# Fetching spilled results earlier, and one weight sum made by an accumulating DMA, in a two-layer float32 encoder

## The chip, the cores and the metric

The kernel runs on one core of a Trainium2 chip. The metric is the device time of one execution in microseconds (us). TensorE (PE in the profile) does the matmuls, with its weight loads shown as PEld; VectorE is DVE, ScalarE is ACT, GpSimd is POOL and SyncE is SP. SP, ACT and POOL also issue DMAs, each in the order of its own instruction queue; an engine that has reached an instruction whose inputs are missing waits there, with everything queued behind it.

## The reference, cut to what matters

Two layers over 256 rows of 2048 channels in float32. Per layer one input projection gives all branches; the branches are gated, projected, mixed and put through an output projection with a residual.

```
h = rmsnorm(x, norm_w)
proj = h @ w_in          # q_m k_m v_m z_m o_m g_m q_r k_r v_r z_r gate_m gate_r
h_m = mlstm(q_m, k_m, v_m, gates), both directions
u_m = head_rmsnorm(sigmoid(o_m) * h_m) * silu(z_m)
h_r = retention(rope(q_r), rope(k_r), v_r), both directions
u_r = head_rmsnorm(h_r) * silu(z_r)
mix = sigmoid([gate_m, gate_r] + b_mix)
y = mix[:D] * (u_m @ w_proj_m) + mix[D:] * (u_r @ w_proj_r)
x = x + y @ w_out
```

## The kernel before, in words

**Matmuls.** Every float32 operand is split into a high part that TensorE takes as it is and a remainder; a product is three matmuls (high by high, high by low, low by high; `mm3`, L270 to L273). Weights stream from DRAM in pieces of 128x1024 (512 KB): `wload` issues the DMA on SP into one of 7 `raw` tiles, `wsplit` lets ScalarE write the high part `whi` (L262) and VectorE the remainder `wlo` (L263), both into one pool of 12 `w` tiles. `gemm` (L332) is one product of 256 rows by 512 columns: 8 pieces of 12 matmuls each.

**Side work.** Seven pairs of 512-column blocks per layer (o_m, gate_m, half of z_r, gate_r) are not done by `gemm` but by `seven` (L411), which needs seven half-size products in the place of eight (a Strassen scheme). Its items are fed out beside the main gemms, by weights: `side_chunk` (L321) is called after each piece of a gemm and takes items until its share of the total weight is reached. Items p1, p5, p6 and p7 load the weight pieces r11, r12 and r22 and make three sums of them on VectorE: r11+r12 in place, that plus r22 into one of the four slices of the tile `keep` (L445), and r12+r22. After `middle` the items p2, p3 and p4 load r21 (and r22 again); p4 adds r21 into the slice of `keep` (the fourth sum, `wsum`, L268) and multiplies with it. `middle` and `end` combine the products, and `finish` applies the gate: for gate_m and gate_r it loads a row of `b_mix` into a `row` tile (2 of them, shared with the decay rows `dec` of the retention) by a DMA on ACT's queue.

**Spills.** Results that are needed later go to DRAM: `spill` (L97) is a DMA on POOL's queue, `fetch` (L102) one on SP's queue into one of 7 tiles of 128x512 (`t512`), which most small steps share.

**Order.** A compiler pass places the instructions of each engine by priority: an instruction's place in the program, less the offset of `tc.high_priority`. Loads, fetches and weight splits carry 800 (`AHEAD`); the vector and scalar operations named `vec` and `sca` carry 1600 (`URGENT`). `later` queues the small steps, and `run_later` takes one step of them at each piece of a gemm from number `lead` on (3 unless said). In the stage of the z_m gemms (named zm) the queue holds `gated` (the product of h_m and sigmoid(o_m), its mean square) and `um_chunk` (transposes of the gated result for the next product). The gemms named pj are the two projections, zr are the direct half of z_r, wo the output projection.

Of the kernel before, what the change touches and what calls it, by code (L numbers as in the profile page):

```python
# [16 lines left out]
P = 128  # L17
# [44 lines left out]
def encoder_kernel(ctx: ExitStack, tc: tile.TileContext, x, x_t, positions, w_main, w_qk0, w_qk1, b_mgate, vecs, b_mix,  # L62
# [12 lines left out]
    def bank(name):  # L75
        return pg.tile([P, 512], F32, name=name, tag="bank")
# [331 lines left out]
            yield  # L408
        side_start(make_items(s_hi=s_hi, s_lo=s_lo, keep=bigt("keep", 4)), 20 * NCK)

    def seven(l, xop, s_hi, s_lo, keep, blk, finish):  # L411

        def sop(i, kt):
            o = (i * HK + kt) * P
# [14 lines left out]
        def p1(i):  # L429
            if i == 0:  # L430
                for name in "abcd":
                    st["ps_" + name] = bank("s" + name)
            load("r11", 0, i)
            load("r12", 1, i)
            load("r22", 1, HC + i)
            product(st["ps_a"], lambda kt: xop(0, kt), st["r11"], i, True, True)
# [5 lines left out]
        def p6(i):  # L442
            with tc.high_priority(offset=AHEAD):
                t2 = keep[:, i * CW:(i + 1) * CW]
                nc.vector.tensor_tensor(out=t2, in0=st["r11"], in1=st["r22"], op=ALU.add)  # L445
            product(st["ps_b"], lambda kt: sop(1, kt), t2, i, True, True)

        def p7(i):
            wsum(st["r12"], st["r12"], st["r22"])
# [14 lines left out]
        def p2(i):  # L464
            if i == 0:
                for name in "acd":
                    st["ps_" + name] = bank("r" + name)
            load("r21", 0, HC + i)
            load("r22", 1, HC + i)
            product(st["ps_a"], lambda kt: xop(0, HK + kt), st["r21"], i, True, True)  # L470
# [3 lines left out]

        def p4(i):
            t2 = keep[:, i * CW:(i + 1) * CW]
            wsum(t2, t2, st["r21"])
            product(st["ps_d"], lambda kt: xop(1, HK + kt), t2, i, True, True)

        def end():  # L480
# [13 lines left out]
                items.append((w, lambda fn=fn, i=i: fn(i)))  # L494
        items.append((2.0, middle))
        for i in range(HC):
            for w, fn in ((0.5, p2), (0.5, p3), (1.6, p4)):
                items.append((w, lambda fn=fn, i=i: fn(i)))
        items.append((1.5, end))
        return items  # L500
# [263 lines left out]
    for l in range(DEPTH):  # L764
# [53 lines left out]

        def side_items(l=l, xop=xop, rs=rs, s_hi=None, s_lo=None, keep=None):
            def finish_with(kind, b0):  # L820
                def finish(t, n, src, own):
                    sg = t512(kind) if own is None else own
                    b = b0 + n
                    if kind in ("om", "zr"):
                        sca.activation(out=sg, in_=src, func=AF.Sigmoid if kind == "om" else AF.Silu, scale=rs[t])
                    else:
                        bm = row("bm")
                        mc = (0 if kind == "gm" else D) + b * NB
                        with tc.high_priority(offset=AHEAD):
                            nc.scalar.dma_start(out=bm, in_=b_mix[l:l + 1, mc:mc + NB].broadcast_to([P, NB]))  # L830
                        vec.scalar_tensor_tensor(out=sg, in0=src, scalar=rs[t], in1=bm, op0=ALU.mult,
                                                       op1=ALU.add)
                        sca.activation(out=sg, in_=sg, func=AF.Sigmoid)
                    spill((kind, l, b, t), sg)
                return finish
            items = []
            for kind, base, b in (("om", B_O_M, 0), ("om", B_O_M, 2), ("gm", B_GATE, 0), ("gm", B_GATE, 2),
                                  ("zr", B_Z_R, 0), ("gr", B_GATE + NBLK, 0), ("gr", B_GATE + NBLK, 2)):
                items += seven(l, xop, s_hi, s_lo, keep, base + b, finish_with(kind, b))
            return items  # L840

        for b in range(NBLK):
# [49 lines left out]
        um = []  # L892

        def gated(h, hs, ss):
            for t in range(NT):
                hv = fetch(("hm", l, h, t), "hm_b")
                so = fetch(("om", l, h, t), "so_b")
                vec.tensor_tensor(out=hv, in0=hv, in1=so, op=ALU.mult)
                sca.activation(out=so, in_=hv, func=AF.Square, accum_out=ss[:, t:t + 1])
                hs.append(hv)  # L900
                yield
            rstd_m = sm.tile([P, NT], F32, name="rstd_m")
            rsqrt_mean(rstd_m, ss, NT, NB)
            hs.append(rstd_m)
# [4 lines left out]
        for b in range(NBLK):  # L909
            side_need(("om", l, b, 1))  # L910
            side_need(("om", l, b, 0))
            hs = []
            ss_m = sm.tile([P, NT], F32, name="ss_m")
            later(gated, b, hs, ss_m)
            ps = gemm(xop, wmain(l, B_Z_M + b), "zm")
            while len(hs) <= NT:
                run_later()
            rstd_m = hs[NT]
            ev = []
            for t in range(NT):  # L920
                z = t512("z")
                sca.activation(out=z, in_=ps[t], func=AF.Silu, scale=rs[t])
                vec.scalar_tensor_tensor(out=z, in0=hs[t], scalar=rstd_m[:, t:t + 1], in1=z,
                                               op0=ALU.mult, op1=ALU.mult)
                ev.append(z)
            later(um_chunk, ev, b)
# [4 lines left out]

        uop = lambda t, kt: in_acts(um)(t, kt)
        for b in range(NBLK):
            ps = gemm(uop, wmain(l, B_PROJ_M + b), "pj")
            for t in range(NT):
                side_need(("gm", l, b, t))
                sg = fetch(("gm", l, b, t), "gm_b")
                vec.tensor_tensor(out=sg, in0=ps[t], in1=sg, op=ALU.mult)
                spill(("ym", l, b, t), sg)

# [2 lines left out]
        def ur_chunk(b, zs):  # L943
            ev = []
            hrs = [fetch(("hr", l, 2 * b + k), "hr_b") for k in range(2)]
            for t in range(NT):
                z = fetch(("zr", l, b, t), "z_b") if zs is None else zs[t]
                for k in range(2):
                    i = t * NH_R + 2 * b + k
                    zk = z[:, k * S:(k + 1) * S]  # L950
                    vec.scalar_tensor_tensor(out=zk, in0=hrs[k][:, t * S:(t + 1) * S], scalar=rstd_r[:, i:i + 1],
                                             in1=zk, op0=ALU.mult, op1=ALU.mult)
                ev.append(z)
            if zs is None:
                yield
            ur[b] = transpose_split(ev, b, None, None, (l, V_RN))
            yield

# [24 lines left out]
        for b in range(NBLK):  # L983
            if b == 2:
# [2 lines left out]
                y_hi, y_lo = bigt("y_hi", 2, F32R), bigt("y_lo", 3, F32R)  # L987
                later(y_chunk, None, 0)
                later(y_chunk, None, 1)
            ps = gemm(rop, wmain(l, B_PROJ_R + b), "pj", lead=2)  # L990
            ev = []
            for t in range(NT):
                side_need(("gr", l, b, t))
                sg = fetch(("gr", l, b, t), "gr_b")
                ym = fetch(("ym", l, b, t), "ym_b")
                vec.tensor_tensor(out=sg, in0=ps[t], in1=sg, op=ALU.mult)
                vec.tensor_tensor(out=sg, in0=ym, in1=sg, op=ALU.add)
                ev.append(sg)
# [181 lines left out]
```

## Time and profile before

| what | value |
|---|---|
| median of 3 runs | 2194.8 us (2194.19 to 5458.12) |
| the profiled execution | 2194.46 us |
| its span, first to last instruction | 2192.4 us |
| TensorE busy | 2154.0 us, 98% of the span |
| VectorE busy | 1813.4 us, 83% |
| ScalarE busy | 1304.3 us, 59% |
| GpSimd busy | 66.9 us, 3% |
| mean DMA rate | 236 GB/s, 518.25 MB moved |

The profiled execution is the one to which the rows below belong; 2.1 us of its time lie outside its span. Matmuls are pipelined, so one matmul's duration in the profile is longer than the distance from its start to the next one's; TensorE's pace is read from the starts.

### The profile page before, as it was taken

To read this page: it belongs to the slowest core of one execution; us is meant where nothing else is said; L and a number is where in the kernel's file an instruction comes from. 1 tells how busy PE (TensorE), PEld (TensorE's weight loads), DVE (VectorE), ACT (ScalarE), POOL (GpSimd) and SP (SyncE) were. 2 spreads that over 40 slices of the span, in tenths; PEclk is the share of its full clock that TensorE was granted. 3 is DMA by queue.
4 is the path that set the end of the run, shared out by engine and by line. 5 is a ranking of instruction groups with operands and counts; after the bars stand their busy time and mean duration, and the time that the engine had idled before them with its cause. 6 is when DMAs were issued, how large, how long until landed. Compare 5 with 4: busy or idle time off the path is not lost.

```text
span 2192.4 us, 28486 instructions
## 1 busy us (share of the span) xinstructions
PE 2154.0 (98%) x10024; PEld 1809.9 (83%) x10024; DVE 1813.4 (83%) x2327; ACT 1304.3 (59%) x1627; POOL 66.9 (3%) x130
## 2 busy tenths in 40 slices
PE   7999999999999999999999999999999999999998
PEld 7988888888778888888899888888887788888887
DVE  6997898897898998985578778989978989889854
ACT  6745466656775656564457555665567656565543
POOL 0000000000000000000000000000000000000000
PEclk9999999999999999999999999999999999999999
DMA  8645577767777887887656456776777778878963
GB/s 277 213 150 190 191 236 236 229 229 241 241 241 264 280 283 258 271 295 276 221 168 208 164 185 210 236 234 216 240 247 239 255 255 292 280 252 277 326 223 125
DMA packets 161071, 518.25 MB, mean 236 GB/s; under 512 B 19616, under 2 KB 22176, under 8 KB 160928
## 3 DMA queue, kind: packets, MB, share of 16 engines
q1 hardware_dynamic: 143552, 471.98, 65.4%
q0 software_dynamic: 9600, 31.46, 3.6%
q10 hardware_dynamic: 7776, 13.00, 2.0%
q8 instruction: 78, 1.28, 0.2%
q14 instruction: 65, 0.53, 0.1%
HBM read 482.81 MB, written 33.55 MB: 236 GB/s over the span
## 4 chain that ended last, share of the span: by engine, by line
issue 48%; PE 42%; DVE 3%; DMA 3%; POOL 2%; ACT 1%; SPq 0%; ACTq 0%; POOLq 0%; DVEq 0%
PE pj L272 3%; PE pj L273 3%; PE pj L271 3%; DVE wlo L263 2%; PE vm L271 1%; PE vm L272 1%; PE wo L273 1%; PE wo L272 1%; PE wo L271 1%; PE vr L271 1%; PE vr L272 1%; PE qr L271 1%; PE vm L273 1%; PE qr L273 1%; PE vr L273 1%
## 5 line engine op out<-in xcount | busy, mean ns | idle before, releaser
L262 ACT CAST whi<-raw 128x1024 fp32r<-128x1024 f32 (+2 forms) x832 | 844.6, 1034 | 608.1 <-DVE raw L268 147.7
L263 DVE TENSOR_TENSOR wlo<-raw,whi 128x1024 fp32r<-128x1024 f32 (+2 forms) x832 | 981.0, 1200 | 214.7 <-ACT whi L262 200.1
L272 PE MATMUL pj<-wlo,u_hi 128*128 128x512 f32 x512 | 199.4, 390 | 0.6 <-DVE wlo L263 0.5
L271 PE MATMUL pj<-whi,u_hi 128*128 128x512 f32 x512 | 199.9, 391 | 0.0
L273 PE MATMUL pj<-whi,u_lo 128*128 128x512 f32 x512 | 199.3, 389 | 0.0
L262 ACT CAST whi<-keep 128x1024 fp32r<-128x1024 f32 x112 | 117.7, 1051 | 60.0 <-PE qr L272 12.8
L263 DVE TENSOR_TENSOR wlo<-keep,whi 128x1024 fp32r<-128x1024 f32 x112 | 136.4, 1218 | 15.7 <-ACT whi L262 15.1
L268 DVE TENSOR_TENSOR raw<-raw 128x1024 f32<-128x1024 f32 x112 | 136.4, 1218 | 0.8
L271 PE MATMUL qk<-whi,ht_hi 128*128 128x384 f32 (+2 forms) x320 | 113.7, 357 | 10.5 <-ACT whi L262 10.5
L272 PE MATMUL qk<-wlo,ht_hi 128*128 128x384 f32 (+2 forms) x320 | 113.4, 354 | 1.0 <-DVE wlo L263 1.0
L272 PEld LDWEIGHTS pj<-wlo,u_hi 128*128 128x128 f32 x512 | 96.1, 188 | 21.0 <-DVE wlo L263 1.5
L273 PE MATMUL qk<-whi,ht_lo 128*128 128x384 f32 (+2 forms) x320 | 113.0, 353 | 0.0
L273 PEld LDWEIGHTS pj<-whi,u_lo 128*128 128x128 f32 x512 | 96.1, 188 | 20.0
L271 PEld LDWEIGHTS pj<-whi,u_hi 128*128 128x128 f32 x512 | 96.0, 188 | 20.0 <-ACT whi L262 0.4
L272 PE MATMUL zm<-wlo,ht_hi 128*128 128x512 f32 x256 | 100.0, 391 | 1.0 <-DVE wlo L263 0.9
L271 PE MATMUL vm<-whi,ht_hi 128*128 128x512 f32 x256 | 100.3, 392 | 0.0
L273 PE MATMUL vm<-whi,ht_lo 128*128 128x512 f32 x256 | 100.2, 391 | 0.0
L271 PE MATMUL vr<-whi,ht_hi 128*128 128x512 f32 x256 | 100.1, 391 | 0.0
L271 PE MATMUL qr<-whi,ht_hi 128*128 128x512 f32 x256 | 100.1, 391 | 0.0
L272 PE MATMUL vm<-wlo,ht_hi 128*128 128x512 f32 x256 | 100.0, 391 | 0.0
L271 PE MATMUL zm<-whi,ht_hi 128*128 128x512 f32 x256 | 100.0, 392 | 0.0
L272 PE MATMUL vr<-wlo,ht_hi 128*128 128x512 f32 x256 | 99.8, 390 | 0.0
(313 smaller groups left out, 4664.6 us busy)
## 6 DMA issues: line engine op xcount, KB each, us to landing
raw<-in_w_main_dram SPq DMA_DIRECT2D x776, 512.0 KB, 5.0
raw<-in_w_qk_dram SPq DMA_DIRECT2D x48, 384.0 KB, 3.2
bm<-in_b_mix_dram ACTq DMA_DIRECT2D x32, 256.0 KB, 4.4
raw<-in_w_qk_dram SPq DMA_DIRECT2D x15, 400.0 KB, 5.2
hm<-hm POOLq DMA_DIRECT2D x16, 256.0 KB, 4.6
om<-c POOLq DMA_DIRECT2D x16, 256.0 KB, 3.5
hr<-hr POOLq DMA_DIRECT2D x16, 256.0 KB, 5.7
gm<-c POOLq DMA_DIRECT2D x16, 256.0 KB, 4.7
```

The lines of the kernel that those rows point to most:

```text
L262: nc.scalar.copy(out=whi, in_=raw)
L263: nc.vector.tensor_tensor(out=wlo, in0=raw, in1=whi.bitcast(F32), op=ALU.subtract)
L268: nc.vector.tensor_tensor(out=dst, in0=a, in1=b, op=ALU.add)
L271: nc.tensor.matmul(out=ps, lhsT=xh, rhs=whi, start=first, stop=False)
L272: nc.tensor.matmul(out=ps, lhsT=xh, rhs=wlo, start=False, stop=False)
L273: nc.tensor.matmul(out=ps, lhsT=xl, rhs=whi, start=False, stop=last)
```

## The change

Four things are edited.

- In `seven`, `p6` issues, right after its product, a DMA on POOL's queue that reads r21 from DRAM and adds it in place into the slice of `keep`; `p4` no longer has the sum, and its weight in the feeding of side items falls from 1.6 to 0.5.
- The `b_mix` rows are loaded once per pair and block (two DMAs on SP's queue) by `early`, called in p1 and p2 of the last piece, in the place of once per `finish` (four DMAs on ACT's queue).
- `gated` and `ur_chunk` fetch all their tiles in one step and use them two steps later; the zm gemms start to take queued steps at piece 1.
- In the two projections the gate tiles (and the `ym` tiles) are fetched ahead of the gemm, with an offset of 60, in the place of behind it with 800.

```diff
+            if i == HC - 1:
+                early(1)
...
             product(st["ps_b"], lambda kt: sop(1, kt), t2, i, True, True)
+            with tc.high_priority(offset=AHEAD):
+                nc.gpsimd.dma_start(out=t2, in_=wmain(l, blk)(HC + i), accum_op=ALU.add)
...
+            if i == HC - 1:
+                early(0)
...
         def p4(i):
             t2 = keep[:, i * CW:(i + 1) * CW]
-            wsum(t2, t2, st["r21"])
             product(st["ps_d"], lambda kt: xop(1, HK + kt), t2, i, True, True)
...
-            for w, fn in ((0.5, p2), (0.5, p3), (1.6, p4)):
+            for w, fn in ((0.5, p2), (0.5, p3), (0.5, p4)):
...
+                def early(n):
+                    if kind in ("gm", "gr"):
+                        bms[n] = row("bm")
+                        mc = (0 if kind == "gm" else D) + (b0 + n) * NB
+                        nc.sync.dma_start(out=bms[n], in_=b_mix[l:l + 1, mc:mc + NB].broadcast_to([P, NB]))
...
-                        bm = row("bm")
-                        mc = (0 if kind == "gm" else D) + b * NB
-                        with tc.high_priority(offset=AHEAD):
-                            nc.scalar.dma_start(out=bm, in_=b_mix[l:l + 1, mc:mc + NB].broadcast_to([P, NB]))
+                        bm = bms[n]
...
         def gated(h, hs, ss):
-            for t in range(NT):
-                hv = fetch(("hm", l, h, t), "hm_b")
-                so = fetch(("om", l, h, t), "so_b")
+            ops = [(fetch(("hm", l, h, t), "hm_b"), fetch(("om", l, h, t), "so_b")) for t in range(NT)]
+            yield from pause(2)
+            for t in range(NT):
+                hv, so = ops[t]
...
-            ps = gemm(xop, wmain(l, B_Z_M + b), "zm")
+            ps = gemm(xop, wmain(l, B_Z_M + b), "zm", lead=1)
...
+            for t in range(NT):
+                side_need(("gm", l, b, t))
+            sgs = [fetch(("gm", l, b, t), "gm_b", 60) for t in range(NT)]
             ps = gemm(uop, wmain(l, B_PROJ_M + b), "pj")
             for t in range(NT):
-                side_need(("gm", l, b, t))
-                sg = fetch(("gm", l, b, t), "gm_b")
+                sg = sgs[t]
...
-            for t in range(NT):
-                z = fetch(("zr", l, b, t), "z_b") if zs is None else zs[t]
+            if zs is None:
+                zs = [fetch(("zr", l, b, t), "z_b") for t in range(NT)]
+                yield from pause(2)
+            for t in range(NT):
+                z = zs[t]
...
+            early = []
+            for t in range(NT):
+                if b < 2:
+                    early.append(fetch(("ym", l, b, t), "ym_b", 60))
+                    continue
+                early.append(fetch(("gr", l, b, t), "gr_b", 60))
             ps = gemm(rop, wmain(l, B_PROJ_R + b), "pj", lead=2)
...
-                sg = fetch(("gr", l, b, t), "gr_b")
-                ym = fetch(("ym", l, b, t), "ym_b")
+                sg = fetch(("gr", l, b, t), "gr_b") if b < 2 else early[t]
+                ym = fetch(("ym", l, b, t), "ym_b") if b >= 2 else early[t]
```

## Rows read from the trace of the kernel before

**Rows 1.** The page, part 1: busy time of each engine and its share.
```profile
PE 2154.0 (98%) x10024; PEld 1809.9 (83%) x10024; DVE 1813.4 (83%) x2327; ACT 1304.3 (59%) x1627; POOL 66.9 (3%) x130
```

**Rows 2.** Waits of PE, whole span: us in total, times, longest.
```profile
PE qk L271 <- ACT whi L262: 10.5, 2, 8.5
PE sd L272 <- DVE wlo L263: 8.4, 4, 4.6
PE ra L272 <- DVE wlo L263: 4.0, 4, 1.8
PE psc L379 <- ACT qkm_hi L119: 2.2, 1, 2.2
...
PE zm L272 <- DVE wlo L263: 0.9, 1, 0.9
...
PE pj L272 <- DVE wlo L263: 0.5, 1, 0.5
PE tr L235 <- DVE z L119: 0.4, 1, 0.4
```

**Rows 3.** Busy time by stage: PE, PEld, DVE, ACT, POOL; granted clock, DMA share, GB/s.
```profile
0.00:35.00 35.00, 23.46 (x105) 22.09 (x106) 19.89 (x43) 26.03 (x51) 1.68 (x10) 0.94 0.90 318
...
570.00:680.00 110.00, 102.80 (x446) 83.32 (x445) 96.96 (x125) 77.24 (x98) 2.72 (x5) 0.97 0.74 245
680.00:800.00 120.00, 120.00 (x535) 99.44 (x534) 104.77 (x102) 68.22 (x72) 5.42 (x10) 1.00 0.83 283
...
1655.00:1765.00 110.00, 102.61 (x449) 82.02 (x448) 99.29 (x126) 77.59 (x96) 2.17 (x4) 1.00 0.74 249
...
2095.00:2192.00 97.00, 88.96 (x442) 75.54 (x440) 50.54 (x69) 38.82 (x54) 0.00 (x0) 0.98 0.48 161
```

**Rows 4.** PE in order of time: start, duration; idle before and its releaser.
```profile
573.17 0.39 PE L271 MATMUL zm<-whi,ht_hi 128*128 128x512 f32 x1
573.40 0.39 PE L272 MATMUL zm<-wlo,ht_hi 128*128 128x512 f32 x1
...
573.85 0.39 PE L271 MATMUL sd<-whi,s_hi 128*128 128x512 f32 x1
578.85 0.79 PE L272 MATMUL sd<-wlo,s_hi 128*128 128x512 f32 x1 [4.61 <-DVE wlo L263]
...
580.29 0.63 PE L272 MATMUL sd<-wlo,s_hi 128*128 128x512 f32 x1
580.72 0.63 PE L273 MATMUL sd<-whi,s_lo 128*128 128x512 f32 x1
```

**Rows 5.** DVE in order of time, the same moment.
```profile
573.37 0.69 DVE L119 TENSOR_TENSOR hm_b<-hm_b,so_b 128x512 f32<-128x512 f32 x1 [2.72 <-DMA so_b<-om]
576.18 0.69 DVE L119 TENSOR_TENSOR hm_b<-hm_b,so_b 128x512 f32<-128x512 f32 x1 [2.12 <-DMA so_b<-om]
576.79 0.87 DVE L119 SCALAR_TENSOR_TENSOR u_lo<-tr,vec_sb,u_hi 128x256 fp32r<-128x256 f32 x2
577.58 1.21 DVE L263 TENSOR_TENSOR wlo<-raw,whi 128x1024 fp32r<-128x1024 f32 x1
```

**Rows 6.** SP's queue in order of time, the fetches of that step.
```profile
568.22 0.33 SPq L105 DMA_DIRECT2D hm_b<-hm  x1
...
569.84 1.10 SPq L105 DMA_DIRECT2D so_b<-om  x1
```

**Rows 7.** Waits of DVE from 550 to 700 us.
```profile
DVE hm_b L119 <- DMA so_b<-om: 10.3, 6, 2.7
```

**Rows 8.** Groups of DVE instructions: busy us, mean ns, idle before and its releasers.
```profile
L263 DVE TENSOR_TENSOR wlo<-raw,whi 128x1024 fp32r<-128x1024 f32 (+2 forms) x832 | 981.0, 1200 | 214.7 <-ACT whi L262 200.1 <-PE tr L235 5.9 <-PE tr L603 1.5
...
L268 DVE TENSOR_TENSOR keep<-keep,raw 128x1024 f32<-128x1024 f32 x56 | 68.3, 1220 | 34.0 <-DMA raw<-in_w_main_dram 34.0
```

**Rows 9.** The tile keep from 570 to 680 us: its fourth sums.
```profile
L268 DVE TENSOR_TENSOR keep<-keep,raw x4: 1214/1216/1217, 622.5 to 648.6; 128x1024 f32<-128x1024 f32 x4
```

**Rows 10.** ACT in order of time at the end of a zm gemm.
```profile
1674.19 1.28 ACT L119 ACT_TABLE_LOAD   x1
1675.49 1.27 ACT L119 ACTIVATE z<-zm,rstd 128x512 f32<-128x512 f32 x2
```

**Rows 11.** DVE in order of time, the step that follows it.
```profile
1677.75 1.41 DVE L119 SCALAR_TENSOR_TENSOR z<-hm_b,rstd_m,z 128x512 f32<-128x512 f32 x2
```

**Rows 12.** DMA queues, and issues: KB each, median us to landing.
```profile
q1 hardware_dynamic: 143552, 471.98, 65.4%
...
raw<-in_w_main_dram SPq DMA_DIRECT2D x776, 512.0 KB, 5.0
...
bm<-in_b_mix_dram ACTq DMA_DIRECT2D x32, 256.0 KB, 4.4
...
y_b<-y SPq DMA_DIRECT2D x8, 256.0 KB, 9.4
```

**Rows 13.** DVE, the last reader of keep's fourth slice in p6, last pair of layer 0.
```profile
925.25 1.22 DVE L263 TENSOR_TENSOR wlo<-keep,whi 128x1024 fp32r<-128x1024 f32 x1
```

**Rows 14.** ACT, the first reader of that slice in p4.
```profile
956.95 1.06 ACT L262 CAST whi<-keep 128x1024 fp32r<-128x1024 f32 x1 [0.31 <-PE rd L272]
```

**Rows 15.** Groups of POOL instructions: the spills of one kind.
```profile
L99 POOL DMA_DIRECT2D ym<-gm_b x16 | 8.7, 544 | 155.4 <-DVE gm_b L119 154.9
```

More of the change, by code (lines that the diff above doesn't have):

```diff
@@ L409, in sums_of_operand, with seven @@
         side_start(make_items(s_hi=s_hi, s_lo=s_lo, keep=bigt("keep", 4)), 20 * NCK)
-    def seven(l, xop, s_hi, s_lo, keep, blk, finish):
+    def seven(l, xop, s_hi, s_lo, keep, blk, finish, early):
         def sop(i, kt):
@@ L820, in finish_with @@
             def finish_with(kind, b0):
+                bms = {}
+                def early(n):
[3 more added lines that the diff above has]
+                        nc.sync.dma_start(out=bms[n], in_=b_mix[l:l + 1, mc:mc + NB].broadcast_to([P, NB]))
                 def finish(t, n, src, own):
@@ L834, in finish @@
                     spill((kind, l, b, t), sg)
-                return finish
+                return finish, early
             items = []
@@ L838, in side_items @@
                                   ("zr", B_Z_R, 0), ("gr", B_GATE + NBLK, 0), ("gr", B_GATE + NBLK, 2)):
-                items += seven(l, xop, s_hi, s_lo, keep, base + b, finish_with(kind, b))
+                items += seven(l, xop, s_hi, s_lo, keep, base + b, *finish_with(kind, b))
             return items
@@ L953, in ur_chunk @@
                 ev.append(z)
-            if zs is None:
-                yield
+            yield
             ur[b] = transpose_split(ev, b, None, None, (l, V_RN))
```

## The prediction, made before the changed kernel was run

> **What bounds the kernel now.** I began with the busy shares: TensorE is busy 98% of the span [rows 1]. Such a share can hide slow matmuls, so I read the pace next: consecutive full matmuls start 0.227 us apart (573.17 and 573.40 [rows 4]), and hold that pace through whole stages. The kernel is bound by TensorE's instruction stream, of which the change removes nothing. What can be won is the time in which TensorE waits, so the third view is its waits [rows 2]. The largest, 10.5 us on the first weights, belongs to the start, where the change does nothing (0 to 35 us [rows 3]); so do the tail (from 2095 us) and the 2.2 us on psc. What is left waits for `wlo`, VectorE's half of a weight split: sd 8.4 us, ra 4.0, zm 0.9, pj 0.5; and 0.4 us of a transpose on z.
>
> The fourth view, busy time by stage, says where: 7.20 us of idle PE between 570 and 680 us and 7.39 us between 1655 and 1765, the z_m gemms of the two layers [rows 3]; from 680 to 800 us TensorE idles 0.00. In those two stages VectorE is busy 96.96 and 99.29 of 110 us. Weight splits run ahead of their matmuls by up to 12 `w` tiles, six pieces; a VectorE that is full uses that lead up, and then any wait of its own reaches TensorE. In the order of time I read the largest, 4.61 us of sd [rows 4]: VectorE stands 2.72 and 2.12 us for `so_b` [rows 5], and the next `wlo` only starts at 577.58. The fetches had been issued at 568.22 to 569.84 [rows 6] and the multiplications stood in VectorE's queue before the data were there. Six such waits take 10.3 us in this stage [rows 7].
>
> **The slow clock.** After that wait matmuls start 0.43 us apart for a while (580.29 and 580.72 [rows 4]), near half pace, and the stage's granted clock is 0.97 [rows 3]: some 6.6 us at 1.2 instead of 2.4 GHz, 3.3 us lost. In the second layer the stage kept 1.00. The Trainium skill, page "TensorE: Matmul & The Clock Gate", section "What's actually happening", says that an idle array falls back to half clock; by it each removed long wait would return a slow stretch as well, 6.6 us in all where these rows give 3.3. The trace shows it once in two, so the sum takes 3.3.
>
> **Part 1, the fourth sum.** Removed: 56 VectorE sums of 1.220 us, 68.3 us in all [rows 8]; VectorE goes from 83% to some 80%. Almost all of it lies beside TensorE's work and is worth nothing there. The four sums of each z_m stage lie from 622.5 to 648.6 us [rows 9] and in the like place of layer 1: 4.9 us of VectorE each, exactly where ra waits. I put the ra waits and pj's at zero: -4.5 us. The 34.0 us that VectorE stood for r21 before these sums [rows 8] also leave its queue; it had been paid out of its lead, so I count nothing. The first sd wait comes before the sums of its stage and is not helped by them directly.
>
> The weight of p4 falls, so a pair's total goes from 4 x 5.3 + 2 + 4 x 2.6 + 1.5 = 35.1 to 30.7. The same 160 calls then give the VectorE-heavy p1 to p7 69% of a pair's time where they had 60%. One round of p1 to p7 is 24 matmuls (5.4 us) and 7 VectorE operations (8.5 us); with its main pieces (12 matmuls and one operation each, 3.45 of them before, 3.95 after) VectorE's load on TensorE's time falls from 86% to 82%, and for p2 to p4 from 80% to 70%. The order has more slack everywhere.
>
> Added: 56 accumulating DMAs on POOL's queue. The trace has none. Issue: spills take 0.544 us of POOL [rows 15]; 56 more are 30 us on an engine that is busy 66.9 [rows 1]. Behind a waiting one stand spills, which nobody needs soon. Landing: nearest is the plain load of the same size on SP, 5.0 us; the longest median of any load here is 9.4 [rows 12]. It must land before p4 casts the slice; the shortest distance in layer 0 between the last reader in p6 and that cast is 956.95 - (925.25 + 1.22) = 30.5 us [rows 13, 14]. So its cost is nothing while it lands within 30 us; with that cover gone ScalarE would stand, and with it every `whi`. DMA time: 471.98 MB on SP's queue, 900 loads of 0.52 MB, fill 65.4% of 2192 us [rows 12], 1.59 us each; 56 at one to three times that are 4 to 12% of the span. The stage from 680 us, the densest one with side work, is at 0.83 [rows 3] and would come to 0.87 to 0.95, not full. Taken: 0.
>
> **Part 2, fetches in `gated` and lead=1.** The sd and zm waits (8.4 + 0.9 us) and the 3.3 us of clock, 12.6 us together, hang on the `so_b` waits. Fetching both halves together and using them two steps later helps if the multiplication stands later in VectorE's queue. That isn't sure: the `vec` operations carry twice the offset of the fetches, so they are pulled up to where the compiler believes the data to be there, and the fetches wait for one of 7 tiles in both versions. The ends are 12.6 and 0; neither row is nearer, and I take half, -6.3 us. The lead of 1 brings `um_chunk`'s transposes two pieces closer to the end of the gemm that makes their input: table load 1.28, two activations 1.27 [rows 10] and two products 1.41 [rows 11], 3.96 us, against one piece of 12 x 0.227 = 2.72 us and the side items after it. At worst 1.24 us at each of 8 gemms, 9.9 us; at best nothing, since the pass can place other matmuls first (the same kind of wait costs 0.4 now [rows 2]). Taken: +1.0.
>
> **Part 3, fetches in `ur_chunk` and the projections, `b_mix` rows.** Their stages idle nearly nothing, so they win the 0.4 us of z. The 32 row loads of 4.4 us [rows 12] become 16, on SP's queue, where they stand between weight loads; 18 matmuls of p5 to p7, 4.1 us, and the main pieces between cover the landing. A fetch that finds no free tile holds the weight loads behind it on SP, but seven raw tiles are 7 x 2.72 = 19 us of main gemm. Taken: 0; bounded by one wait like the 4.61 us in each layer, 9.2 us.
>
> **Sum**, against the profiled execution: 2194.46 - 4.5 - 0.4 - 6.3 + 1.0 = 2184.3, predicted 2184. The median shown is 0.3 us higher, which is nothing here.
>
> **Rivals.**
> - *The waits are only moved* (22%): the multiplications are pulled up as before, the `so_b` waits and the slow stretch stay. For it: the offsets, and fetches that are issued 5 to 6 us before use [rows 5, 6], no longer than such a landing takes. Against: VectorE has more lead to pay with. 2194.46 - 4.9 + 1.0 = 2191.
> - *All of it goes* (10%): VectorE's added slack alone swallows what waits remain. 2194.46 - 4.9 - 12.6 = 2177.
> - *Slots become the wait* (11%): four of 7 tiles held by `gated`, two more by a projection, both `row` tiles by `b_mix` while retention wants `dec`. With part 3's 9.2 us and no gain of part 2: 2194.46 - 4.9 + 9.2 + 1.0 = 2200.
> - *The accumulating DMA lands too late* (7%), the one that ends on the other side. It pays from 30.5 us on, and reaches TensorE after another six pieces of splits, 6 x 6 x 0.227 = 8.2 us. At 45 us: 14 pairs x (45 - 30.5 - 8.2) = 88 us, 2283. For it: reading and rewriting the slice is work that no row prices. Against: it would have to be five times the 9.4 us above.
> - The forecast itself has 50%.
>
> **Range and chances.** 2172 to 2206: the low end is the 2177 of the rival less the psc and like waits, which a new order may lose by luck; the high end is no gain in part 2 with the whole 9.9 us of transposes and a little more. It leaves out the late DMA and some luck, about one in ten. A difference under 2%, 44 us, is about what a measurement of this kernel can tell from no change. All TensorE waits that the change can touch, with the clock, are some 18 us, so faster by over 2% is nearly excluded: 0.02. Slower by over 2% is the late DMA: 0.07. Within 2%: 0.91.
>
> **What the profile after would show.** The L268 sums of keep gone (56 fewer on VectorE, some 68 us) and POOL with 56 more issues; VectorE's busy time in the z_m stages some 5 us lower; ra waits gone. For part 2: no `hm_b` waits for `so_b` over 1 us, no sd wait, granted clock 1.00 in that stage; if they stand there, the first rival. ACT waiting for the DMA of `keep` would be the slow rival; `tr` waiting for z, the lead. The prediction is wrong if TensorE's pace itself moves, or if new waits of over 10 us appear in stages that have none.

## The result, and the profile after

The changed kernel takes 2217.66 us (median of 4 runs, 2215.84 to 2218.99) against 2194.49 us in the same session: a ratio of 1.011, 95% interval 1.009 to 1.013. It is some 23 us slower, where 10 us less had been predicted, and it lies 12 us above the range. The profiled execution took 2217.93 us with a span of 2216.2 us.

The page of the changed kernel: busy time, two DMA queues (packets, MB, share of the 16 engines' time), and three issues (KB each, median us to landing).

```profile
PE 2162.0 (98%) x10024; PEld 1815.8 (82%) x10024; DVE 1758.5 (79%) x2271; ACT 1300.5 (59%) x1621; POOL 117.5 (5%) x186
...
q1 hardware_dynamic: 145856, 476.17, 63.7%
q0 software_dynamic: 17664, 60.83, 11.2%
...
raw<-in_w_main_dram SPq DMA_DIRECT2D x776, 512.0 KB, 5.3
keep<-in_w_main_dram POOLq DMA_DIRECT2D x56, 512.0 KB, 8.4
...
bm<-in_b_mix_dram SPq DMA_DIRECT2D x16, 256.0 KB, 3.9
```

VectorE has its 56 instructions less and GpSimd its 56 issues more [rows 1]. The issues cost (117.5 - 66.9) / 56 = 0.90 us each, where a spill takes 0.54 [rows 15]. The accumulating DMA lands in 8.4 us, well within the 30.5 us of cover [rows 13, 14]. Weight loads land in 5.3 us, before in 5.0 [rows 12].

The waits of the changed kernel, for the lines that answer to [rows 2] and [rows 7] (here whole span).

```profile
POOL keep L450 <- DVE wlo L263: 549.6, 44, 20.9
ACT whi L262 <- DMA raw<-in_w_main_dram: 79.5, 39, 8.9
DVE hm_b L119 <- DMA so_b<-om: 20.8, 9, 3.6
PE sc L272 <- DVE wlo L263: 15.0, 7, 5.3
PE tr L235 <- DMA y_b<-y: 12.5, 2, 6.5
```

The ra waits are gone. The wait of the z_m stages is still there, now at sc; the waits for `so_b` still stand at 20.8 us. New are 12.5 us on `y_b`, once in each layer. ScalarE waits 79.5 us for weight loads where it waited 34.2 before; the 34.0 us for which VectorE had stood for r21 [rows 8] are gone.

By stage, first the kernel after, then the kernel before for the two stretches that [rows 3] does not have.

```profile
570.00:680.00 110.00, 109.41 (x484) 89.60 (x483) 95.83 (x119) 78.11 (x94) 6.61 (x9) 0.99 0.85 267
680.00:800.00 120.00, 117.56 (x513) 96.61 (x512) 95.67 (x94) 66.49 (x69) 10.03 (x15) 0.99 0.87 286
925.00:1012.00 87.00, 79.75 (x348) 65.17 (x347) 64.44 (x67) 45.31 (x50) 5.09 (x9) 0.94 0.87 294
1655.00:1765.00 110.00, 104.00 (x458) 85.15 (x457) 95.39 (x123) 76.44 (x98) 6.17 (x9) 0.98 0.83 270
2010.00:2110.00 100.00, 94.00 (x416) 77.78 (x415) 76.66 (x80) 53.30 (x58) 6.17 (x10) 0.97 0.88 298
```

```profile
925.00:1012.00 87.00, 86.84 (x396) 71.92 (x395) 69.85 (x74) 46.65 (x51) 4.34 (x8) 1.00 0.90 314
2010.00:2110.00 100.00, 100.00 (x459) 83.13 (x458) 77.96 (x82) 52.89 (x58) 3.44 (x7) 1.00 0.86 295
```

In a kernel at full pace a count of matmuls is a measure of progress, a rough one here, since a few of the instructions are short transposes. From 925 to 1012 us TensorE starts 48 fewer than before, from 2010 to 2110 us 43 fewer; at 0.227 us these are 10.9 and 9.8 us, some 21 of the 23.8 us that the span grew. The earlier stages gain and lose too (38 more from 570 to 680 us, 22 fewer from 680 to 800), but counted from the start the changed kernel is level at 925 us (4185 against 4187) and 51 behind at 1012. Both stretches are the end of the last gate pair and the middle of the second projection. The granted clock is 0.94 and 0.97, where it was 1.00. The DMA share of the z_m stages went from 0.74 [rows 3] to 0.85 and 0.83.

TensorE in order of time, at the wait of the first of these stretches:

```profile
983.10 0.39 PE L272 MATMUL pj<-wlo,u_hi 128*128 128x512 f32 x1
983.33 0.39 PE L273 MATMUL pj<-whi,u_lo 128*128 128x512 f32 x1
990.26 0.69 PE L235 MATMUL tr<-ident,y_b 128*128 128x128 f32 x2 [6.55 <-DMA y_b<-y]
```

SP's queue there, first after, then before:

```profile
976.51 0.33 SPq L105 DMA_DIRECT2D gr_b<-gr  x1
977.25 3.06 SPq L251 DMA_DIRECT2D raw<-in_w_main_dram  x5
980.40 0.62 SPq L105 DMA_DIRECT2D gr_b<-gr  x1
981.43 3.96 SPq L105 DMA_DIRECT2D y_b<-y  x4
```

```profile
955.21 8.53 SPq L251 DMA_DIRECT2D raw<-in_w_main_dram  x5
963.79 3.09 SPq L105 DMA_DIRECT2D y_b<-y  x4
```

The y tiles, which the transposes for the output projection need, are fetched at 981.43, behind the early gate fetches, where they were fetched at 963.79. Where the product of `gated` waits, the changed kernel looks like the old one [rows 4, 5]. VectorE, then TensorE:

```profile
566.21 0.69 DVE L119 TENSOR_TENSOR hm_b<-hm_b,so_b 128x512 f32<-128x512 f32 x1 [2.65 <-DMA so_b<-om]
566.81 2.35 DVE L263 TENSOR_TENSOR wlo<-raw,whi 128x1024 fp32r<-128x1024 f32 x2
```

```profile
568.09 0.79 PE L272 MATMUL sc<-wlo,s_hi 128*128 128x512 f32 x1 [4.37 <-DVE wlo L263]
568.68 0.63 PE L273 MATMUL sc<-whi,s_lo 128*128 128x512 f32 x1
569.11 0.63 PE L271 MATMUL sc<-whi,s_hi 128*128 128x512 f32 x1
```

After the wait of 4.37 us matmuls start 0.43 us apart, the half pace that was seen in the old kernel at 580 us.

### The profile page after: what moved, and what is told of

Its sections match the earlier page's. It is cut to its first block, busy times and chain, and to the rows that moved or that the text cites. A ratio compares the mean times of both kernels' runs of the same rounds, so it can differ in the third digit from the quotient of the medians.

```text
span 2216.2 us, 28574 instructions
## 1 busy us (share of the span) xinstructions
PE 2162.0 (98%) x10024; PEld 1815.8 (82%) x10024; DVE 1758.5 (79%) x2271; ACT 1300.5 (59%) x1621; POOL 117.5 (5%) x186
## 3 DMA queue, kind: packets, MB, share of 16 engines
q0 software_dynamic: 17664, 60.83, 11.2%
q10 hardware_dynamic: 3168, 4.61, 0.6%
## 4 chain that ended last, share of the span: by engine, by line
issue 49%; PE 43%; POOL 4%; DMA 3%; ACT 1%; DVE 1%; POOLq 0%; SPq 0%; ACTq 0%; DVEq 0%
PE vm L272 3%; PE vm L271 3%; PE wo L272 3%; PE wo L271 3%; PE wo L273 3%; PE vm L273 3%; PE qk L271 2%; PE qk L273 2%; PE qk L272 2%; PE qr L273 2%; PE qr L271 2%; PE qr L272 2%; POOL keep L450 2%; PE vr L272 1%; PE vr L271 1%
## 5 line engine op out<-in xcount | busy, mean ns | idle before, releaser
L263 DVE TENSOR_TENSOR wlo<-keep,whi 128x1024 fp32r<-128x1024 f32 x112 | 136.6, 1219 | 13.2 <-ACT whi L262 10.4
L273 PE MATMUL zm<-whi,ht_lo 128*128 128x512 f32 x256 | 100.4, 392 | 0.0
```

The costliest lines, as they stand in the source:

```text
L263: nc.vector.tensor_tensor(out=wlo, in0=raw, in1=whi.bitcast(F32), op=ALU.subtract)
L273: nc.tensor.matmul(out=ps, lhsT=xl, rhs=whi, start=False, stop=last)
```

## The experiments

The expectations name theories by letters. A: the early projection fetches stand on SP's queue, waiting for their own spills or tiles, and hold weight loads and y fetches behind them. B1: the accumulating DMA loads the 16 DMA engines, so weight loads come late. B2: the new order and weight of the side items. B3: spills queue behind it on GpSimd. C: the queued steps come too early (lead=1). D: the 7 tiles of 128x512 are held too long. E: the offset of 1600 pulls `gated`'s products in front of their data. F: the order in which the fetches are asked for. Ratios are to the kernel before on the same chip, in brackets the 95% interval.

**One part at a time.** First the projections' fetches: taken back out of the changed kernel, and put alone into the old one.

```diff
-            sgs = [fetch(("gm", l, b, t), "gm_b", 60) for t in range(NT)]
...
-                    early.append(fetch(("ym", l, b, t), "ym_b", 60))
...
-                early.append(fetch(("gr", l, b, t), "gr_b", 60))
```

> The changed kernel with the fetches of both projections put back behind their gemms (offset 800), all else changed. Theory A (the fetches placed ahead of the projections stand on SP's queue until their own spills have landed, and hold weight loads and the y fetches behind them): the 12.5 us of transposes waiting for y_b and the waits of 668 to 692 us go, with their slow stretches, 2185 to 2192 us. Theory B (the accumulating DMA costs it, by fuller DMA engines or by spills that stand behind it on POOL's queue): 2210 to 2218. Theory C (the earlier queued steps of the zm gemms cost it): 2210 to 2218.

Measured: 2209.18 us, 1.006 [1.0041, 1.0079]: some 17 us over theory A, 1 us under B and C.

> The kernel before with the fetches of both projections ahead of their gemms and nothing else changed. Theory A: 2210 to 2220 us, with y_b waited for by the transposes. Theories B and C: 2190 to 2197, as before.

Measured: 2207.59 us, 1.006 [1.0044, 1.0076], between the two expectations. The fetches alone cost some 13 us; without them 15 of the 23 us remain. So there are two losses.

Next, the old kernel with the accumulating DMA and the weight of 0.5 alone:

```diff
+                nc.gpsimd.dma_start(out=t2, in_=wmain(l, blk)(HC + i), accum_op=ALU.add)
-            wsum(t2, t2, st["r21"])
-            for w, fn in ((0.5, p2), (0.5, p3), (1.6, p4)):
+            for w, fn in ((0.5, p2), (0.5, p3), (0.5, p4)):
```

> The kernel before with the fourth sum made by the accumulating DMA and the weight of p4 at 0.5, nothing else. Theory A: 2186 to 2192 us, the ra waits of the z_m stages gone, the first sd wait there. Theory B: 2208 to 2220.

Measured: 2215.64 us, 1.0097 [1.0078, 1.0116], the largest loss of any part, as theory B expected. And `gated` and `ur_chunk` in two steps with lead=1, exactly as in the diff of the change:

```diff
+            ops = [(fetch(("hm", l, h, t), "hm_b"), fetch(("om", l, h, t), "so_b")) for t in range(NT)]
+            yield from pause(2)
...
+            ps = gemm(xop, wmain(l, B_Z_M + b), "zm", lead=1)
```

> The kernel before with the fetches of gated and ur_chunk two steps ahead and the zm gemms starting at piece 1, nothing else. Theory A: 2188 to 2197 us; if the multiplications are pulled up as before, the so_b waits stay at some 19 us in all. Theory C: 2208 to 2220, from new waits of the transposes or slots.

Measured: 2194.0 us, 1.0000 [0.999, 1.0011]: nothing, so theory C falls. Alone, the parts cost 21.5 + 13.4 + 0 us, together 23: they do not add. In part both lie in the same stretch: from 925 to 1012 us sum_only, too, starts fewer matmuls than the old kernel, 364 against 396.

**The sum, taken apart.** The kernel without the fourth sum (neither VectorE nor a DMA adds r21, so `keep` lacks it) shows what the removal wins at the weight of 0.5; the next one loads r21 over the slice by a plain DMA in the place of adding it (the addition is left out); then the weight alone, with the sum on VectorE; then the accumulating DMA with the old weight.

```diff
-            wsum(t2, t2, st["r21"])                                # no_sum: weight 0.5, no DMA
+                nc.gpsimd.dma_start(out=t2, in_=wmain(l, blk)(HC + i))   # plain_dma
+            for w, fn in ((0.5, p2), (0.5, p3), (0.5, p4)):               # w05_only, with the wsum
+                nc.gpsimd.dma_start(out=t2, in_=wmain(l, blk)(HC + i), accum_op=ALU.add)   # sum_w16, with (1.6, p4)
```

> The kernel before without the fourth sum: p4 multiplies with the slice of keep as p6 left it (the addition of r21 is left out), the weight of p4 is 0.5, no DMA is added. If the loss of the sum's part comes from the accumulating DMA (theory B1: its 3.0 us of all 16 DMA engines, twice a plain load's, delay the fetches and weight loads that are in flight): 2183 to 2190 us, faster than before. If it comes from the new order that the weight 0.5 and the missing sums give (theory B2): 2205 to 2216.

> The kernel with the sum's part alone, but the DMA on POOL's queue overwrites the slice in the place of adding to it (the addition is left out): the same bytes from DRAM, the same waits and places, no reading of the slice. Theory B1: half of the loss is gone or more, 2195 to 2205, with half the time on the DMA engines. If spills standing behind these DMAs on POOL's queue were the cost (theory B3): as with the accumulating DMA, 2210 to 2217. Theory B2: the same 2210 to 2217.

> The kernel before with the weight of p4 at 0.5 and the sum still made by VectorE. Theory B1: within 8 us of before, some way up since VectorE's sums then stand closer together. Theory B2: 2205 to 2216.

> The kernel before with the accumulating DMA and the weight of p4 left at 1.6. Theory B1 and B3: the loss stays, 2207 to 2218. Theory B2: it goes, 2190 to 2196.

| kernel | us | ratio | ACT waits for raw, us |
|---|---|---|---|
| no_sum | 2188.22 | 0.9974 [0.9963, 0.9985] | 27.5 |
| plain_dma | 2201.8 | 1.0034 [1.0024, 1.0043] | 55.8 |
| sum_only | 2215.64 | 1.0097 [1.0078, 1.0116] | 92.3 |
| w05_only | 2202.35 | 1.004 [1.0026, 1.0054] | 27.6 |
| sum_w16 | 2200.48 | 1.0024 [1.0013, 1.0034] | 81.3 |

Waits of ScalarE for weight loads: no_sum, plain_dma, sum_only, one line of each. Then GpSimd's DMA queue of no_sum and of plain_dma.

```profile
ACT whi L262 <- DMA raw<-in_w_main_dram: 27.5, 19, 6.0
```

```profile
ACT whi L262 <- DMA raw<-in_w_main_dram: 55.8, 32, 5.6
```

```profile
ACT whi L262 <- DMA raw<-in_w_main_dram: 92.3, 43, 6.6
```

```profile
q0 software_dynamic: 9600, 31.46, 3.6%
```

```profile
q0 software_dynamic: 17664, 60.83, 7.8%
```

No_sum and plain_dma came as theory B1 expected; w05_only (within 8 us of before, or 2205 to 2216) and sum_w16 (2207 to 2218, or 2190 to 2196) met neither expectation.

At the weight of 0.5 and without the sum the kernel gains 0.26% on the old one, 5.8 us: that is the ceiling of this part at this weight. The plain DMA costs 0.6% on top, some 13 us, and the addition as much again: 27 us for 56 DMAs of 512 KB, all at the weight of 0.5. From the shares a plain one takes (0.078 x 2199.5 - 0.036 x 2192.4) / 56 = 1.66 us of all 16 engines (the 3.6% stand in the old kernel too), an accumulating one, with the 11.2% of the changed kernel, (0.112 x 2216.2 - 78.9) / 56 = 3.02 us: 1.8 times as much for the same bytes. In these three kernels the time, the engines' time and ScalarE's waits rise together; GpSimd's queue has the same 56 instructions in plain_dma and sum_only, so the second half of the loss is not B3. In the first half spills behind the DMA could have a share; that was not separated.

The weight is a cost of its own. With VectorE's sum the 0.5 costs 8.3 us, and with the DMA it makes 15 us of difference (2200.48 against 2215.64). By the feeding, p2 to p4 get 6.0 of 30.7 of a pair's calls in the place of 10.4 of 35.1, 20% for 30%, for the same eight side loads, so those come closer together. That this is the reason is argued, not shown. What the traces show is the place: in the stretches of 925 to 1012 and 2010 to 2110 us together sum_only starts 60 matmuls fewer than the old kernel, 13.6 us at 0.227, and w05_only 52; sum_w16 starts 1 fewer, no_sum 3. The first stretch of sum_only, then of sum_w16:

```profile
925.00:1012.00 87.00, 82.69 (x364) 66.90 (x363) 67.44 (x73) 45.95 (x51) 5.32 (x9) 0.98 0.90 314
```

```profile
925.00:1012.00 87.00, 86.79 (x395) 71.83 (x394) 65.53 (x70) 46.58 (x51) 5.25 (x9) 1.00 0.91 317
```

So late loads are no price by themselves. In sum_w16 ScalarE waits for them nearly as long as in sum_only, and its traced execution, the fastest of its ten, took 2193.16 us, no more than the old kernel's (what it loses in the others, median 2200.48, was not traced). The loss of this part is one of the DMA and the weight together; how the late loads become waits of TensorE at 0.5 and hardly at 1.6 is not shown, and no run leaves out the sum at 1.6, which would price the DMA alone there. But even with the old weight the part does not win (1.0024).

One moment of late transfers in the trace of sum_only, across four engines: GpSimd, SP, VectorE, TensorE.

```profile
587.07 0.88 POOL L448 DMA_DIRECT2D keep<-in_w_main_dram  x1 [14.10 <-DVE wlo L263]
```

```profile
590.02 0.65 SPq L105 DMA_DIRECT2D so_b<-om  x1
```

```profile
598.08 0.69 DVE L119 TENSOR_TENSOR hm_b<-hm_b,so_b 128x512 f32<-128x512 f32 x1 [4.67 <-DMA so_b<-om]
```

```profile
599.96 0.79 PE L272 MATMUL zm<-wlo,ht_hi 128*128 128x512 f32 x1 [3.35 <-DVE wlo L263]
```

The DMA goes out just ahead of four tile fetches that were issued with weight loads around them; `so_b` arrives 8 us after its issue, VectorE stands 4.67 us, and TensorE 3.35. The old kernel has a wait of this kind too (4.61 us of TensorE [rows 4, 5]), so the moment shows a path, not the size of the loss.

**The second projection.** The early fetches of both projections on GpSimd's queue, so that they can't stand on SP's; then those of the second projection alone on SP.

```diff
-            nc.sync.dma_start(out=dst, in_=spilled[key])
+            (nc.sync if early == AHEAD else nc.gpsimd).dma_start(out=dst, in_=spilled[key])
```

> The kernel with the projections' part alone, but the fetches that were placed ahead of the gemms are issued on POOL's queue in the place of SP's; their tiles are held for the same stretch. Theory A (a fetch that waits for its spill or for a tile stands on SP's queue in front of weight loads and of the y fetches): the loss goes, 2191 to 2198 us, and the transposes no longer wait for y_b. Theory D (the 7 shared tiles are held too long, whoever issues the fetch): the loss stays, 2203 to 2210.

Measured: 2210.09 us, 1.0062 [1.0045, 1.0079]. The loss stays, with waits of 10.8 us for `y_b`: theory A falls, and the time is theory D's, at its upper end.

> The kernel before with the early fetches of the second projection (ym and gr) alone, those of gm as before. Theory A: the y_b waits with their slow stretches (some 10 us) are there and the waits at 675 to 695 us are not, 2201 to 2206 us. If the first projection's gm fetches are what costs: 2193 to 2198.

Measured: 2207.73 us, 1.0054 [1.0039, 1.0069], 2 us over theory A's range. The first projection's fetches cost nothing that shows; the loss is the second one's. Next the same without the early gr fetches of blocks 2 and 3, and the same with 9 tiles (and 6 raw tiles, to make room) beside its own reference.

```diff
-                early.append(fetch(("gr", l, b, t), "gr_b", 60))          # gr_late
...
-        return tmp.tile([P, 512], dtype, name=name, tag="t512", bufs=7)   # rproj_slots, slots9
+        return tmp.tile([P, 512], dtype, name=name, tag="t512", bufs=9)
-        raw = wp.tile([P, CW], F32, name="raw", tag="raw", bufs=7)[:, 0:n]
+        raw = wp.tile([P, CW], F32, name="raw", tag="raw", bufs=6)[:, 0:n]
```

> The kernel before with the early ym fetches of the second projection's blocks 0 and 1 alone; gr is fetched behind the gemm as before. Theory D (the early gr fetches of blocks 2 and 3 hold tiles of the pool of 7 while they wait for their own spills, so the y tiles come late): the loss of 12 us is gone, 2193 to 2198 us, PE waits for y_b under 2 us in all, and the y_b fetches are issued before 970 us in layer 0. Rival (any fetch ahead of that gemm costs, since it holds tiles through the gemm): 2203 to 2208 us.

Measured: 2198.45 us, 1.0016 [1.0006, 1.0025], at the end of theory D's range and with no wait for `y_b`. Three quarters of the loss hang on the early gr fetches. SP's queue of rproj_only, then of gr_late:

```profile
962.10 17.36 SPq L251 DMA_DIRECT2D raw<-in_w_main_dram  x10
979.56 2.01 SPq L105 DMA_DIRECT2D gr_b<-gr  x2
981.68 2.86 SPq L105 DMA_DIRECT2D y_b<-y  x4
```

```profile
960.84 4.87 SPq L251 DMA_DIRECT2D raw<-in_w_main_dram  x4
965.77 2.20 SPq L105 DMA_DIRECT2D y_b<-y  x4
```

> The kernel before with 9 tiles of 128x512 and 6 raw tiles, the reference point for the run above. All theories: a raw tile less shortens the lead of the weight loads, 2194 to 2203 us; if it is over 2210 the loads were short of tiles already, and then the run above can tell little.

> The second projection's early fetches (ym and gr), with 9 tiles of 128x512 in the place of 7 and, to make room, 6 raw tiles in the place of 7. Read against slots9, which has the same tiles and the fetches of before. Theory D: the two added tiles let the y fetches go, so most of the 12 us is gone, at most 4 us above slots9, and PE waits for y_b under 4 us. Rival (the order of the instructions around that gemm has moved, and the tiles do not matter): 8 to 14 us above slots9, PE waits for y_b of 10 us as in the run with 7 tiles.

Measured: slots9 2224.21 us, 1.0137 [1.0119, 1.0155]; rproj_slots 2227.34 us, 1.0149 [1.0134, 1.0164]. The difference of 3 us meets theory D's number, but slots9 lies over the 2210 beyond which it tells little, and the wait itself speaks against D. Waits of rproj_slots, and its queue on SP:

```profile
PE tr L235 <- DMA y_b<-y: 12.1, 2, 6.5
```

```profile
959.85 24.94 SPq L251 DMA_DIRECT2D raw<-in_w_main_dram  x13
984.89 1.15 SPq L105 DMA_DIRECT2D gr_b<-gr  x2
986.13 3.20 SPq L105 DMA_DIRECT2D y_b<-y  x4
```

With two tiles more the y fetches still stand behind gr, and behind more loads. This led to theory F. In the compiled order of SP's queue the weight loads ahead of the first y fetch can be counted: 381 in the old kernel and in gr_late, 387 in rproj_only and in the changed kernel; 380 in slots9, 386 in rproj_slots; in proj_pool, whose early gr fetches are not on SP's queue at all, it is 385. The program asks for the gr tiles first, so the y fetches are placed six loads later. At one load per 2.72 us of main gemm these are some 16 us, and the traces show a shift of 18 (963.79 to 981.68). To test it y is asked for first:

```diff
-            if ev is None:
-                ev = [fetch(("y", l, b, t), "y_b") for t in range(NT)]
-                yield
...
-                later(y_chunk, None, 0)
-                later(y_chunk, None, 1)
+                for q in range(2):
+                    later(y_chunk, [fetch(("y", l, q, t), "y_b") for t in range(NT)], q)
```

> The second projection's early fetches (ym and gr) with 7 tiles, and the y fetches of blocks 0 and 1 asked for in the program ahead of the early gr fetches of block 2, in the place of in the first queued step behind them. Theory F (the early gr fetches are asked for before y and so put the y fetches six weight loads later in SP's queue): y is issued before 968 us in layer 0, PE waits for y_b under 2 us, 2194 to 2200 us. Theory D (the early gr tiles hold the pool of 7 while they wait for their spills): y takes four of the 7 tiles first, so the gr fetches now wait longer than before, and the loss stays, 2203 to 2210 us.

Measured: 2203.7 us (2196.76 to 2208.06), 1.0035 [1.0021, 1.005]. The count is 381 again and y is issued at 964.74, as F says; the waits are shorter, and from 940 to 1010 us the clock is 1.00 where rproj_only had 0.95. Waits of y_first:

```profile
PE tr L235 <- DMA y_b<-y: 4.3, 3, 2.1
```

Yet theory F's time and wait are not met, and the time lies just within theory D's range: the median came down by a third of the loss, and the interval overlaps that of rproj_only. That the order puts the y fetches later is shown by the counts; that it makes the whole loss is not. In layer 1 the stretch from 2010 us still starts 21 matmuls fewer than the old kernel, and its clock is 0.98:

```profile
2010.00:2110.00 100.00, 98.13 (x438) 81.08 (x437) 77.14 (x82) 51.44 (x55) 4.32 (x8) 0.98 0.82 279
```

The edit also moves the transposes, since it takes one queued step out of `y_chunk`: in TensorE's order the first of y stands behind 4388 instructions, where it stands behind 4400 in the old kernel and 4437 in rproj_only. Twelve matmuls are 2.7 us less for the tiles to land, more than the longest wait of 2.1 us. Whether this holds the rest, some 8 us with runs that spread over 11, or the held tiles of theory D do, stays open.

**The products of `gated`.** The product and the mean square are emitted without the offset of 1600, with lead=1 and with lead=2.

```diff
-                vec.tensor_tensor(out=hv, in0=hv, in1=so, op=ALU.mult)
-                sca.activation(out=so, in_=hv, func=AF.Square, accum_out=ss[:, t:t + 1])
+                nc.vector.tensor_tensor(out=hv, in0=hv, in1=so, op=ALU.mult)
+                nc.scalar.activation(out=so, in_=hv, func=AF.Square, accum_out=ss[:, t:t + 1])
```

> The kernel with the part of gated and ur_chunk alone, and in gated the product and the mean square without their offset of 1600, so that the compiler keeps them where the program has them. If the offset is what pulls the products in front of their data (theory E): the hm_b waits for so_b fall from 17.8 us to under 6, the sb waits of the z_m stages go, 2184 to 2190 us. If the fetches are late because of the 7 tiles (theory D): waits and time as before, 2192 to 2197.

> As the last, with the zm gemms taking queued steps from piece 2 in the place of 1, the latest start at which all six steps still fit. Theory E, and the transposes waiting for z (5.6 us with the start at piece 1) as the cost of the early start: 2180 to 2187 us, tr no longer waiting for z. If that wait has another cause: the same time as the last one.

Measured: 2189.19 us, 0.9967 [0.9955, 0.998], as theory E expected, and 2187.95 us, 0.9969 [0.9956, 0.9982], 1 us over its range. Waits for `so_b` in gated_only, gated_late and gated_late2:

```profile
DVE hm_b L119 <- DMA so_b<-om: 17.8, 8, 3.6
```

```profile
PE tr L235 <- DVE z L119: 13.2, 6, 3.7
DVE hm_b L899 <- DMA so_b<-om: 12.1, 8, 3.7
```

```profile
DVE hm_b L899 <- DMA so_b<-om: 4.6, 6, 1.1
...
PE tr L235 <- DVE z L119: 0.7, 2, 0.3
```

Theory E holds in the main, and theory D, by which waits and time would stay, falls: two steps of distance in the program do nothing while the offset pulls the product forward, and without the offset the kernel gains some 7 us. The waits for `so_b` fall less than was expected with lead=1 (12.1 us, not under 6) and to 4.6 with lead=2; lead=2 with the offset was not run. In gated_late2 both z_m stages have a clock of 1.00. lead=1 costs the transposes 13.2 us of waits for z, which lead=2 takes to 0.7. The time hardly tells the two apart.

**Combinations.** gated_late2 with the `b_mix` rows on SP's queue, and this with the early gm and ym fetches besides:

```diff
+                        nc.sync.dma_start(out=bms[n], in_=b_mix[l:l + 1, mc:mc + NB].broadcast_to([P, NB]))
...
+            sgs = [fetch(("gm", l, b, t), "gm_b", 60) for t in range(NT)]
...
+            early = [fetch(("ym", l, b, t), "ym_b", 60) for t in range(NT)] if b < 2 else []
```

> The kernel with the later products in gated and lead 2 (2187.95 us, 0.9969 of before), and the b_mix rows loaded once per pair and block on SP's queue in addition. If the b_mix edit costs nothing, as the prediction took it: 2186 to 2190 us, ratio 0.996 to 0.998. If the rows on SP's queue hold weight loads while they wait for a row tile: 2190 to 2196 us, with SP waits for a row tile of over 3 us in all and PE waits for wlo near the ends of the gate pairs.

> The kernel with the later products in gated, lead 2 and the b_mix rows on SP's queue (2185.86 us, 0.996 of before), and in addition the first projection's early gm fetches and the second's early ym fetches, without the early gr fetches and without the accumulating DMA. If these fetches cost nothing: 2184 to 2188 us, ratio 0.995 to 0.997. If they hold tiles that others need: 2188 to 2194 us, ratio 0.997 to 1.000, the rest of what the run with the early ym fetches alone lost (0.16%).

Measured: gl2_bm 2185.86 us, 0.996 [0.9945, 0.9975]; mended 2186.33 us, 0.9959 [0.9946, 0.9972]. The `b_mix` edit costs nothing, and so, here, do the gm and ym fetches, though gr_late alone had shown 0.16%. Both beat the old kernel by some 9 us; they and gated_late2 can't be told apart.

## Why the prediction was wrong, point by point

- **The bound** was read rightly: the pace of 0.227 us per matmul is unchanged. Of the 23.8 us by which the span grew, TensorE's idle time makes 15.8 (38.4 us before, 54.2 after); the rest fits the slow clock behind the waits (mean granted clock 0.990, before 0.995).
- **Part 1, what goes away**: the ra waits went, as put. The 5.8 us of no_sum are near the 4.5 by luck, since they hold the weight of 0.5 too: at that weight the sum on VectorE costs 14.1 us (2202.35 against 2188.22), and no run shows what it costs at 1.6. "Worth nothing" beside TensorE's work did not hold there.
- **Part 1, the accumulating DMA "taken: 0"**: this step failed. At the weight that the change has it measured some 27 us between no_sum and sum_only; at the old weight DMA and removed sum together cost some 6 us (sum_w16). Its numbers were not bad: 3.02 us of the engines lies within the one to three times 1.59 us, the stage from 680 us came to 0.87, the landing kept to its cover. Wrong was what followed: "not full" at a mean of 0.87, and a cost only if the DMA itself comes late. The price is paid by others: weight loads land later (5.0 us in no_sum, 5.5 in sum_only). Whether their lateness reaches TensorE depends on the order, as sum_w16 shows. "The densest one with side work" was also misread: from 925 to 1012 us the old kernel is at 0.90 and has side work, and there the loss came. That the loads have little to spare can be seen in slots9: one raw tile of seven less, with two more tiles of 128x512 and nothing made scarcer but the raw tiles, costs 29 us (2224.21 against 2195.5). The prediction counted the seven tiles as 19 us of cover for anything.
- **The weight of p4 as "more slack everywhere"**: failed. VectorE's load per piece was worked out, that of the weight loads was not; the weight alone costs 8.3 us, 15 with the DMA, and with the old weight the two stretches of the loss are as before (1 matmul fewer).
- **Part 2, -6.3 + 1.0**: the first rival was right, and to its reason: the products are pulled up, the waits for `so_b` stay. Alone the part gives 0.0. With the offset gone as well it gives some 7 us, not far from the 6.3; but the 6.3 was half of two ends and came from no row. The transposes' waits for z were 5.6 us in gated_only, within the 0 to 9.9.
- **Part 3, "taken: 0; bounded by 9.2"**: failed by its size and its mechanism. It costs 13.4 us, nearly all in the second projection (rproj_only, some 12), and three quarters of that with the early gr fetches. The prediction had a fetch without a tile hold the loads; what the runs show is y fetches placed behind the early gr fetches and six loads further on, and TensorE waiting for y 6.8 us in rproj_only and 12.5 us in the changed kernel, with a slow stretch behind. How much of the loss the place in the queue makes is open, since y_first won back a third of it. The bound took one wait of 4.61 us a layer and no clock. The `b_mix` rows were rightly put at nothing.
- **The rivals**: "slots become the wait" named the right place, a projection's early fetches, at 2200 us; it lacked the loads. None of the rivals had the DMA's price on others; the slow one looked at its landing alone.
- **Range and signs**: the 0.91 for a time within 2% came true, but not by the prediction's path. Its own sign of being wrong came: 12.5 us of waits for `y_b` in a stage that had next to none. And a kernel like this can be told apart far below the 2% that it allows: the intervals here are 0.1 to 0.2% wide to either side.

## What to carry to other kernels

A DMA that takes work off an engine is priced by the time that it takes from the DMA engines and by the slack of the transfers beside it: look at the densest stretch and at what one buffer less would cost, before a mean share of 0.87 is called room. Waits of an engine that is not the bottleneck do not measure the loss: two kernels with 92 and 81 us of them differed by 15 us. An edit that changes the order beside it has to be priced with it and without it. A fetch moved ahead of use is placed in a queue with others, and it may move those; count in the compiled order what stands ahead of the next fetch that matters. Distance in the program helps only when the consumer isn't given a priority that undoes it.

## What the runs showed of the hardware

The accumulating DMA takes 3.02 us of all 16 engines for 512 KB, a plain one from the same queue 1.66, a plain load on SP 1.59; landing takes 8.4 us, 7.0 and 5.0 to 5.7. The Trainium skill, page "DMA: Bandwidth & Descriptors", section "SDMA does more than copy", lists the addition as a reduction of two streams inside the DMA engines. These runs put it at 1.8 times a copy. The Trainium skill, page "DMA: Bandwidth & Descriptors", section "Issuing engines are not separate DMA queues", says that DMAs of all issuing engines run on the same 16 engines and interleave. The trace agrees: with 56 DMAs on GpSimd's queue the median landing of the loads on SP's queue goes from 5.0 us (no_sum) to 5.2 (plain_dma) and 5.5 (sum_only).

The granted clock fell after the 6.55 us wait for `y_b` (0.94 in that stretch) and after the 3.0 us wait of rproj_only (0.95 from 940 to 1010 us). In y_first the stretch of layer 0, with a wait of 2.1 us, kept 1.00, and that of layer 1, with one of 1.8 us, came to 0.98; in the old kernel the stage from 1655 us, with a wait of 2.8 us, kept 1.00 [rows 3]. So in these runs the length of a wait alone does not tell whether a slow stretch follows.
